# Attention in pairs of heads of two groups on halves of the array, with TensorE's order written by hand

## The chip, the cores and the metric

The kernel runs on one core of a Trainium2 chip. TensorE (PE) multiplies into PSUM, VectorE (DVE), ScalarE (ACT) and GpSimd (POOL) do the rest, and SyncE (SP) issues the loads. The metric is the device time of one execution in microseconds (us); lower is better.

## The reference

It is one layer of a decoder trunk on 512 tokens of width 1024: RMSNorm, one wide input projection, three branches (RG-LRU, native sparse attention, gated linear attention), a gated merge, an output projection and a SwiGLU network. The change is in the attention, of 16 heads of width 64 in 4 groups of 4; the heads of a group share keys and values. Each head has three branches with their own keys and values, added under gates:

```python
logit_c = einsum("bgrsd,bgcd->bgrsc", q, kc) + bias_c            # 31 compressed blocks
o_cmp = softmax(where(valid_c, logit_c, NEG_INF)) * valid_c @ vc
o_slc = softmax(q @ k_slc + bias, causal) @ v_slc                # all earlier blocks at this length
o_win = softmax(q @ k_win + bias, window of 256) @ v_win
o = g[0] * o_cmp + g[1] * o_slc + g[2] * o_win                   # g = sigmoid(gate)
```

## The kernel before

All products keep float32 precision: weights and activations are split into a high and a low part, and `mm3` adds three products of parts (high by high, high by low, low by high), at 512 moving columns for most. Weights come in pieces of 128x1024 numbers (`piece`): SP loads one, ACT makes the high part (line 93), POOL during the attention the low part (line 94), three buffers of each.

The stage that the change touches lasts from about 98 to 413 us. It runs over 4 groups `g`, 4 blocks `qb` of 128 queries and 2 pairs `rp` of heads of the group: 32 steps of two heads each. A block has `n1` = 128, 256, 384 or 512 selected keys, `nw` = 128 to 384 keys of the window and 32 compressed ones; the last two kinds are scored together, in `n2` = `nw` + 32 columns. One step is:

- `att_scores`, for each head: two products into bank `s1` and two into `s2` (lines 550 and 551). The stationary operand is the queries, high part over low part, on all 128 rows of the array; the keys move, and their high part stands twice, once for each half of the rows. The second product, queries' high part by keys' low part, has only the 64 rows of the group's half (`half`). Then for each branch DVE adds the bias and takes the maximum (line 558, which frees the bank), and ACT takes the exponential with its sum (line 560). DVE makes the reciprocal of the sums, times the gate (lines 562 and 563), and scales the selected probabilities and the compressed ones (lines 568 and 571), POOL those of the window (line 570).
- `att_out`, of the step before: PE transposes the probabilities in blocks of 128x128 (lines 597 and 602) into one of two `pt` banks, DVE or, each third time, ACT copies them out (`psb`, line 606), and the products with V (lines 620 and 623) use 64 columns of the array each: selected blocks on the left half, window and compressed ones on the right half, 256 columns of two heads at once. ACT and DVE add the halves (lines 635 and 636).
- `fill`: between these stand steps of other projections from `feed` (keys, values and queries of the later groups and the merge gates: 9 jobs of 16 steps, a step being three products of 512 columns, or six of 256 in the values' job). A job takes both banks of `pg` and is copied out at its end.

The program only gives priorities by the order of the code; a scheduler puts each engine's instructions in order. PSUM has 8 banks: 2 in `pg` (projections), 3 in `pa` (scores), 2 in `pt` (transposes), 1 in `po` (sums of V).

Of the kernel before, what the change touches and what calls it, by code (L numbers as in the profile page):

```python
# [22 lines left out]
EV = 3  # L23
# [11 lines left out]
# Distance lines: entry j is the bias at distance JMAX - j (WMAX - j in the window's), NEG where masked.  # L35
# [4 lines left out]
ORDER = "sos"  # L40
RATE = [0.8, 0.8, 0.8, 0.8]
NBIAS, NP1, NP2 = 4, 4, 3
# [11 lines left out]
def bias_select():  # L54
    """[33, LINE + WLINE] one-hot rows: which bucket (or the mask row 32) each line entry takes."""
# [9 lines left out]
def hybrid_block_kernel(ctx, tc, x, rel_table, norm_g, w_in, conv_w, conv_b, lru_w_gates, lru_b_gates,  # L65
# [59 lines left out]
    def psum_t(pools=None):  # L125
        return [p.tile([128, S], F32, name="gps", tag=t) for p, t in (pools or ((pg, "g"), (pg, "g")))]

    def psum_tok():
        ps = [pg.tile([128, 2, 256], F32, name="gps", tag="g") for _ in range(2)]
        return [ps[tb // 2][:, tb % 2] for tb in range(TB)]  # L130

    def steps_t(ps, pc_, kh, act):
        (h, l), (ah, al) = pc_, act
        for n in range(2):
            c = slice(n * 128, n * 128 + 128)
            for k in range(4):
                mm3(ps[n], h[:, k, c], l[:, k, c], ah[:, kh * 4 + k], al[:, kh * 4 + k],
# [3 lines left out]
    def steps_tok(ps, pc_, kh, act):  # L141
        (h, l), (ah, al) = pc_, act
        for tb in range(TB):
# [25 lines left out]
    def gemm_tok(ch, act):  # L169
        """Four [128 tokens, 256 columns] tiles."""  # L170
# [25 lines left out]
    def rstd_of(ss, n, pool):  # L196
        """(ss / n + EPS) ** -0.5, one Newton step on top of the table's square root."""
# [29 lines left out]
    pg = psum_ctx.enter_context(tc.tile_pool(name="pg", bufs=2, space=PSUM))  # L227
    pa = psum_ctx.enter_context(tc.tile_pool(name="pa", bufs=3, space=PSUM))
# [216 lines left out]
    def feed(jobs):  # L445
# [12 lines left out]
        for i, (jb, kh) in enumerate(todo):  # L458
# [5 lines left out]
            if kh:  # L464
                evac(ps)
# [755 lines left out]
```

## Time and profile before

| | us |
|---|---|
| median of 3 runs (lowest, highest) | 1343.72 (1341.64, 1348.01) |
| span of the profiled execution | 1345.8 |
| PE busy in it | 1309.2 (97%) |
| attention in it, from 98 to 413 us | 315.0 |
| in the attention: PE, DVE, ACT, POOL busy | 309.8, 214.1, 170.5, 83.8 |

The table is read by stages: the share of busy time is a mean, and the change is in one stage. A busy PE is not a PE at its peak, since an instruction's length includes its way through the array and what it waits for there. What an instruction takes from PE is the distance from its start to the next start.

### The profile page before, as it was taken

The page shows a single profiled execution, that of the slowest core. Times are in us where ns is not written, and L with a number is a line of the kernel's source. Part 1 is how long each engine was busy: PE and PEld are TensorE (multiplying, and loading weights), DVE is VectorE, ACT ScalarE, POOL GpSimd, SP SyncE. Part 2 cuts the span into 40 slices and gives each one's busy share as a digit, 9 for nine tenths or more (in the row PEclk, how much of TensorE's full clock was granted, in tenths as well). Part 3 has the DMA queues.
Part 4 walks back from the last instruction along what each step waited for, and adds up shares of the span by engine and source line. Part 5 has one row for each costly group of instructions (what it writes and reads, how often), then busy time and mean ns, then how long its engine had stood idle before and what let it go on. Part 6 is the DMA issues. An engine that isn't in the chain of part 4 may idle for free.

```text
span 1345.8 us, 17422 instructions
## 1 busy us (share of the span) xinstructions
PE 1309.2 (97%) x6648; PEld 1038.9 (77%) x6648; DVE 675.3 (50%) x1362; ACT 558.5 (41%) x1057; POOL 332.8 (25%) x219
## 2 busy tenths in 40 slices
PE   7999999999999999989999999999999999999997
PEld 6885556655557877878998888889998888887886
DVE  6536867566667799774333212444743333331114
ACT  4335555456755555844342323323433232231222
POOL 1221323232231454223122133220112222222220
PEclk9998999989999989989999999999999999999999
DMA  7920211103112222333222233534223333332331
GB/s 233 272 67 16 87 32 32 32 16 86 32 33 72 79 71 78 98 94 76 68 78 78 79 94 94 163 103 151 86 75 98 94 94 94 94 99 89 97 105 66
DMA packets 139716, 117.97 MB, mean 88 GB/s; under 512 B 8338, under 2 KB 129406, under 8 KB 139632
## 3 DMA queue, kind: packets, MB, share of 16 engines
q1 hardware_dynamic: 139040, 115.81, 29.4%
q8 instruction: 52, 0.85, 0.3%
q10 hardware_dynamic: 592, 1.05, 0.2%
q14 instruction: 32, 0.26, 0.1%
HBM read 114.67 MB, written 2.17 MB: 87 GB/s over the span
## 4 chain that ended last, share of the span: by engine, by line
PE 81%; DVE 11%; issue 3%; ACT 3%; POOL 2%; DMA 0%; DVEq 0%; ACTq 0%; POOLq 0%
PE gps L163 24%; PE gps L166 12%; PE gps L121 7%; PE gps L123 6%; PE gps L122 6%; PE ops L623 3%; PE acc L121 3%; PE acc L122 3%; PE s L551 3%; PE acc L123 3%; PE ptp L602 3%; PE s L550 3%; DVE xc L822 1%; DVE p L568 1%; DVE wlo L94 1%
## 5 line engine op out<-in xcount | busy, mean ns | idle before, releaser
L94 POOL TENSOR_TENSOR wlo<-wraw,whi 128x1024 fp32r<-128x1024 f32 x90 | 220.2, 2447 | 634.1 <-ACT whi L93 352.1
L93 ACT CAST whi<-wraw 128x1024 fp32r<-128x1024 f32 x177 | 185.3, 1050 | 408.3 <-PE gps L166 262.9
L163 PE MATMUL gps<-hh,whi 128*128 128x512 f32 x704 | 278.2, 396 | 5.6 <-ACT whi L93 3.0
L166 PE MATMUL gps<-hl,whi 128*128 128x512 f32 x704 | 277.1, 394 | 0.0
L94 DVE TENSOR_TENSOR wlo<-wraw,whi 128x1024 fp32r<-128x1024 f32 x87 | 113.7, 1308 | 271.6 <-PE gps L163 148.4
L163 PE MATMUL gps<-hh,wlo 128*128 128x512 f32 x704 | 175.7, 392 | 4.4 <-DVE wlo L94 4.4
L163 PEld LDWEIGHTS gps<-hh,whi 128*128 128x128 f32 x704 | 134.3, 191 | 35.2 <-ACT whi L93 3.9
L163 PEld LDWEIGHTS gps<-hh,wlo 128*128 128x128 f32 x704 | 133.1, 189 | 32.6 <-DVE wlo L94 4.8
L166 PEld LDWEIGHTS gps<-hl,whi 128*128 128x128 f32 x704 | 134.2, 191 | 28.8 <-issue 1.1
L560 ACT ACTIVATE p<-p,mx 128x384 f32<-128x384 f32 (+3 forms) x128 | 69.8, 546 | 67.9 <-DVE mx L558 66.6
L121 PE MATMUL gps<-whi,hh 128*128 128x256 f32 x320 | 94.0, 294 | 0.8 <-DVE kl L475 0.8
L122 PE MATMUL gps<-wlo,hh 128*128 128x256 f32 x320 | 93.1, 291 | 0.0
L123 PE MATMUL gps<-whi,hl 128*128 128x256 f32 x320 | 91.8, 287 | 0.0
L121 PE MATMUL gps<-hh,whi 128*128 128x512 f32 (+1 forms) x184 | 79.4, 436 | 2.6 <-ACT hh L223 1.5
L163 PE MATMUL gps<-yh,whi 128*128 128x512 f32 x192 | 75.7, 394 | 2.7 <-ACT whi L93 2.7
L166 PE MATMUL gps<-yl,whi 128*128 128x512 f32 x192 | 75.4, 393 | 0.0
L121 PE MATMUL acc<-whi,ah 128*128 128x512 f32 x176 | 68.6, 390 | 0.8 <-DVE fsg L1140 0.8
L123 PE MATMUL gps<-hh,wlo 128*128 128x512 f32 (+1 forms) x184 | 68.6, 374 | 0.0
L122 PE MATMUL gps<-hl,whi 128*128 128x512 f32 (+1 forms) x184 | 68.6, 374 | 0.0
L123 PE MATMUL acc<-whi,al 128*128 128x512 f32 x176 | 68.5, 389 | 0.0
L122 PE MATMUL acc<-wlo,ah 128*128 128x512 f32 x176 | 68.5, 389 | 0.0
L570 POOL TENSOR_TENSOR p<-p,sc 128x768 f32<-128x768 f32 (+2 forms) x32 | 40.4, 1264 | 104.1 <-DVE sc L563 74.7
(320 smaller groups left out, 2273.9 us busy)
## 6 DMA issues: line engine op xcount, KB each, us to landing
wraw<-in_w_in_dram SPq DMA_DIRECT2D x68, 512.0 KB, 3.8
wraw<-in_w_ffn_in_dram SPq DMA_DIRECT2D x88, 256.0 KB, 3.2
wraw<-in_w_ffn_out_dram SPq DMA_DIRECT2D x22, 512.0 KB, 3.7
wraw<-in_w_in_dram SPq DMA_DIRECT2D x32, 256.0 KB, 3.1
wraw<-in_w_branch_dram SPq DMA_DIRECT2D x16, 512.0 KB, 3.4
wraw<-in_w_branch_dram SPq DMA_DIRECT2D x16, 256.0 KB, 4.1
wraw<-in_w_out_dram SPq DMA_DIRECT2D x8, 512.0 KB, 3.5
bias<-line_d SPq DMA_DIRECT2D x12, 256.0 KB, 4.3
```

The costliest lines, as they stand in the source:

```text
L93: a_.copy(hi, raw)
L94: lo_eng.tensor_tensor(lo, raw, f(hi), op=OP.subtract)
L121: pe.matmul(ps, lh, rh, start=first, stop=False)
L122: pe.matmul(ps, lh, rl, start=False, stop=False)
L123: pe.matmul(ps, ll, rh, start=False, stop=last)
L163: pe.matmul(ps[n], part_[:, k, c], ah[:, kk], start=kk == 0 and part_ is h, stop=kk == 7 and part_ is l)
L166: pe.matmul(ps[n], h[:, k, c], al[:, kk], start=False, stop=False)
L550: pe.matmul(s[:, :n], q[:, r, qs], kh[:, sl], start=True, stop=False)
L551: pe.matmul(s[:, :n], q[half, r, qs], kl[half, sl], start=False, stop=True)
L560: a_.activation(o, o, AF.Exp, scale=-1.0, bias=mx[:, br, j:j + 1], accum_out=sm[:, br, j:j + 1])
L570: g_.tensor_tensor(w_, w_, sc[:, 2][:, :, None].to_broadcast([128, 2, nw]), op=OP.mult)
L602: pe.transpose(tps[:, hf, j], src[:, j], ident)
```

## The change

It pairs heads in another way. A step now has one head `r` of two groups, 2`gp` and 2`gp`+1. The queries of the first stand in rows 0 to 63, those of the second in rows 64 to 127, high and low part in two tiles; the keys stand once (`KH`, `KL`), the first group's in the upper half of the rows and the second's in the lower. Each score bank takes three products of 64 rows instead of one of 128 and one of 64, and the two heads' products alternate on the two halves of the rows, each head into its own bank: 12 products of one shape (64 rows, 128 columns) in a row. In `att_out` each head has its half of the array's columns for all three branches, 128 moving columns at a time, all products of a step in a row of one shape (128 rows, 64 columns); the compressed ones use the full 128 rows with a mask in `VC`. The sums of the four query blocks of a pair of heads stay in one bank and are copied out once (line 621), so nothing is left to add. The compressed probabilities have four fixed tiles `PC`, set to zero once.

POOL now scales the selected probabilities too. The steps run over 2 pairs of groups, 4 heads and the blocks in the order 0, 3, 1, 2. TensorE's order is that of the code (`manual_schedule`): scores of step i, V products of step i - 2, half of the filling steps, then the transposes of step i - 1 with the other filling steps between. `RATE` is 4.6 filling steps to a step. The banks are 1 in `pg`, 4 in `pa`, 2 in `pt`, 1 in `po`: a projection tile is copied out after 8 filling steps, and the next one uses the same bank. Three pieces of weights are loaded ahead instead of two, and the queries' weights come in four loads of 64 columns instead of one of 256. Biases are loaded per pair of heads.

```diff
-ORDER = "sos"
-RATE = [0.8, 0.8, 0.8, 0.8]
-NBIAS, NP1, NP2 = 4, 4, 3
+QORD = (0, 3, 1, 2)
+RATE = 4.6
+NQ, NP1, NP2, NPSB, NBIAS = 4, 3, 3, 5, 4
...
-    pg = psum_ctx.enter_context(tc.tile_pool(name="pg", bufs=2, space=PSUM))
-    pa = psum_ctx.enter_context(tc.tile_pool(name="pa", bufs=3, space=PSUM))
+    pg = psum_ctx.enter_context(tc.tile_pool(name="pg", bufs=1, space=PSUM))
+    pa = psum_ctx.enter_context(tc.tile_pool(name="pa", bufs=4, space=PSUM))
...
+        for i, (segs, evac, tok) in enumerate(jobs):
+            two = pcs[2 * i:2 * i + 2]
+            for n in range(2):
+                ps = pg.tile([128, S], F32, name="gps", tag="g")
...
+                evac(ps, n)
...
+    def k_evac(gp):
+        def evac(ps, n):
+            c = slice((0, S + 32)[n], (S, 2 * S + 32)[n])
+            a_.copy(KH[gp][:, c], ps)
+            v_.tensor_tensor(KL[gp][:, c], ps, f(KH[gp][:, c]), op=OP.subtract)
...
-                pe.matmul(s[:, :n], q[:, r, qs], kh[:, sl], start=True, stop=False)
-                pe.matmul(s[:, :n], q[half, r, qs], kl[half, sl], start=False, stop=True)
...
+        for s, sl, n in ((s1, slice(0, n1), n1), (s2, sl2, n2)):
+            for i, (qp, kk) in enumerate(((0, kh), (0, kl), (1, kh))):
+                for gi, h in enumerate(HALF):
+                    pe.matmul(s[gi][:, :n], q[h, qp, qs], kk[h, sl], start=i == 0, stop=i == 2)
...
-        for j in range(2):
-            v_.tensor_scalar(p1[:, j, :n1], p1[:, j, :n1], sc[:, 1, j:j + 1], None, op0=OP.mult)
-        w_ = p2[:, :, :nw]
-        g_.tensor_tensor(w_, w_, sc[:, 2][:, :, None].to_broadcast([128, 2, nw]), op=OP.mult)
...
+        for o, br, n in ((p1[:, :, :n1], 1, n1), (p2[:, :, :nw], 2, nw)):
+            g_.tensor_tensor(o, o, sc[:, br][:, :, None].to_broadcast([128, 2, n]), op=OP.mult)
...
-                    pe.matmul(oo, VV[gp][:, kb, c:c + 64], psb[:, hf], start=rp == 0 and i_ == 0, stop=last)
...
+                    v, m = VV[gp][:, kb, c:c + 64], p[:, gi]
+                pe.matmul(ops[h, qb * 128:qb * 128 + 128], v, m, start=first and i == 0,
+                          stop=last and i == len(blocks) - 1)
+        if last:
+            v_.tensor_copy(yb[:, gp, r].rearrange("p (b c) -> p b c", b=TB),
+                           ops.rearrange("p (b c) -> p b c", b=TB)[:, :, ::-1])
...
+    with tc.manual_schedule(engines={mybir.EngineType.PE}):
+        for i in range(len(its) + 2):
+            if i < len(its):
+                gp, r, qb = its[i]
+                probs[i] = att_scores(*its[i])
...
+            if i >= 2:
+                att_out(*its[i - 2], turned.pop(i - 2))
+            quota += RATE
+            n = int(quota)
+            quota -= n
+            for _ in range((n + 1) // 2):
+                next(work, None)
+            n -= (n + 1) // 2
+            if 0 < i <= len(its):
+                turned[i - 1] = []
+                for _ in att_turn(*its[i - 1], probs.pop(i - 1), turned[i - 1]):
+                    if n:
+                        n -= 1
+                        next(work, None)
```

PE, before, in a block with 512 selected keys of the second pair of groups: a head's scores, one filling step (lines 121 to 123), V products of two blocks, transposes.

```order
L550 MATMUL s_2833<-kh_248,q 128x512
L551 MATMUL s_2833<-kl_250,q 128x512
L550 MATMUL s_2834<-kh_248,q 128x416 [waits DVE_49]
L551 MATMUL s_2834<-kl_250,q 128x416
L121 MATMUL gps<-hh,whi 128x512
L122 MATMUL gps<-hl,whi 128x512
L123 MATMUL gps<-hh,wlo 128x512
L623 MATMUL ops<-psb,vv_252 64x256 [waits DVE_49]
L623 MATMUL ops<-psb,vv_252 64x256
L602 MATMUL ptp<-ident,p_2705 128x128 [waits PE_49]
L602 MATMUL ptp<-ident,p_2705 128x128
```

PE, after, in a block with 384 selected keys: the second half of a step's scores, then all V products of an earlier step (line 618; `kh` and `kl` are the keys' parts, `vv` and `vc` the values).

```order
L555 MATMUL s_1505<-kh_247,q 128x416
L555 MATMUL s_1506<-kh_247,q 128x416
L555 MATMUL s_1505<-kl_249,q 128x416
L555 MATMUL s_1506<-kl_249,q 128x416
L555 MATMUL s_1505<-kh_247,q 128x416
L555 MATMUL s_1506<-kh_247,q 128x416
L618 MATMUL ops<-psb,vv_251 64x128 x8
L618 MATMUL ops<-psb,vv_251 64x128 [waits Activation_49]
L618 MATMUL ops<-psb,vv_251 64x128 x3
L618 MATMUL ops<-psb,vv_251 64x128 [waits DVE_49]
L618 MATMUL ops<-psb,vv_251 64x128
L618 MATMUL ops<-psb,vc 64x128 x2
```

The shapes no longer alternate: six products of 64 rows follow each other, two heads by turns, and then 16 of 64 columns.

DVE, before, at the end of a step: a copy of transposes, the reciprocal, the scaling, and the first bias of the next step.

```order
L606 COPY psb<-ptp 128x512 [waits PE_49]
L562 RECIPROCAL sc<-sm 128x6 [waits Activation_49]
L563 TENSOR_TENSOR sc<-sc,gates 128x6 [waits DVE_49]
L568 TENSOR_SCALAR p_2705<-p_2705,sc 128x384 [waits DVE_49]
L610 COPY psb<-ptp 64x128 [waits PE_49]
L568 TENSOR_SCALAR p_2705<-p_2705,sc 128x384
L571 TENSOR_TENSOR pc<-pc,sc 128x2x23
L558 ISA p_2788,mx<-s_2795,bias 128x512 [waits PE_49]
```

DVE, after, at the end of a step.

```order
L567 RECIPROCAL sc<-sm 128x6 [waits Activation_49]
L569 TENSOR_TENSOR sc<-sc,gates 128x6 [waits DVE_49]
L575 TENSOR_TENSOR pc_255<-pc_255,sc 128x2x15 [waits DVE_49]
L600 COPY psb<-ptp 128x512 [waits PE_49] x2
L600 COPY psb<-ptp 128x384 [waits PE_49]
L564 ISA p_1498,mx<-s_1503,bias 128x384 [waits PE_49,Pool_49]
```

The two scalings of line 568 are gone, and all three copies of the transposes of the step before now stand behind the reciprocal, which waits for ACT's exponentials.

ACT, before, where a tile of keys of the later groups (line 473) is copied out of the projection's bank, between the exponentials of two heads.

```order
L560 ACTIVATE p_1471,sm<-p_1471,mx 128x512 [waits DVE_49]
L560 ACTIVATE p_1472,sm<-p_1472,mx 128x384 [waits DVE_49]
L560 ACTIVATE pc,sm<-pc,mx 128x31 [waits DVE_49]
L473 CAST kh_248<-gps 64x512 [waits PE_49]
L560 ACTIVATE p_1471,sm<-p_1471,mx 128x512 [waits DVE_49]
L560 ACTIVATE p_1472,sm<-p_1472,mx 128x384 [waits DVE_49]
L560 ACTIVATE pc,sm<-pc,mx 128x31 [waits DVE_49]
```

ACT, after, where such a tile (line 471) is copied out: the exponentials of both heads of step 5 stand ahead of it.

```order
L566 ACTIVATE p_1322,sm<-p_1322,mx 128x512 [waits DVE_49,Activation_49]
L566 ACTIVATE p_1322,sm<-p_1322,mx 128x512 [waits DVE_49]
L566 ACTIVATE p_1323,sm<-p_1323,mx 128x384 [waits DVE_49] x2
L566 ACTIVATE pc_257,sm<-pc_257,mx 128x31 [waits DVE_49] x2
L471 CAST kh_248<-gps 128x512 [waits PE_49]
L600 COPY psb<-ptp 128x128 [waits PE_49]
```

PE, after, at the same place: the last of the eight filling steps of that tile, then the first of the next tile, which uses the same bank and so waits for DVE's part of the copying out; behind it stand transposes of step 4.

```order
L121 MATMUL gps<-hh,whi 128x512
L122 MATMUL gps<-hl,whi 128x512
L123 MATMUL gps<-hh,wlo 128x512
L121 MATMUL gps<-hh,whi 128x512 [waits DVE_49]
L122 MATMUL gps<-hl,whi 128x512
L123 MATMUL gps<-hh,wlo 128x512
L595 MATMUL ptp<-ident,p_1236 128x128 [waits Pool_49]
L595 MATMUL ptp<-ident,p_1236 128x128
```

The copying out has moved behind the whole step's exponentials, and in PE's fixed order the next tile stands right behind the one that is to be copied out.

## Rows read from the trace of the kernel before

**Rows 1.** The page of the profile, its first part: for each engine busy time, share of the span and instructions (PE is TensorE, DVE VectorE, ACT ScalarE, POOL GpSimd).

```profile
PE 1309.2 (97%) x6648; PEld 1038.9 (77%) x6648; DVE 675.3 (50%) x1362; ACT 558.5 (41%) x1057; POOL 332.8 (25%) x219
```

**Rows 2.** Busy time by stretch: start and end, length, then busy time (and instructions) of PE, its weight loads, DVE, ACT and POOL, the granted clock, and the share and rate of the DMA. The attention, and two stretches inside it in which the clock was at its lower level.

```profile
98.00:413.00 315.00, 309.75 (x1508) 186.97 (x1507) 214.09 (x686) 170.50 (x489) 83.78 (x77) 0.96 0.14 40
...
262.60:276.30 13.70, 13.59 (x39) 8.56 (x40) 6.71 (x29) 5.83 (x20) 1.30 (x2) 0.50 0.16 39
395.70:399.20 3.50, 3.50 (x16) 1.57 (x14) 1.71 (x10) 2.85 (x7) 0.00 (x0) 0.51 0.25 87
```

**Rows 3.** The timeline of PE alone, 12 us in the middle of the attention: start, length, line, out<-in, rows*columns of the array, then the columns that move (the last number of 128x512). The time that an instruction takes from PE is the difference of two starts, since the lengths overlap.

```profile
300.55 0.51 PE L550 MATMUL s<-kh,q 128*128 128x512 f32 x1
300.99 0.49 PE L551 MATMUL s<-kl,q 64*128 64x512 f32 x1
301.41 0.45 PE L550 MATMUL s<-kh,q 128*128 128x416 f32 x1
301.79 0.45 PE L551 MATMUL s<-kl,q 64*128 64x416 f32 x1
302.17 0.50 PE L121 MATMUL gps<-hh,whi 128*128 128x512 f32 x1
302.51 0.40 PE L122 MATMUL gps<-hl,whi 128*128 128x512 f32 x1
302.74 0.39 PE L123 MATMUL gps<-hh,wlo 128*128 128x512 f32 x1
302.98 1.03 PE L602 MATMUL ptp<-ident,p 128*128 128x128 f32 x8
303.77 0.47 PE L121 MATMUL gps<-hh,whi 128*128 128x512 f32 x1
...
308.50 0.40 PE L123 MATMUL gps<-hh,wlo 128*128 128x512 f32 x1
308.83 0.65 PE L623 MATMUL ops<-psb,vv 128*64 128x256 f32 x4
309.41 0.30 PE L597 MATMUL ptp<-ident,pc 128*64 128x128 f32 x1
...
311.12 0.44 PE L620 MATMUL ops<-psb,vc 64*64 64x128 f32 x4
311.48 0.50 PE L550 MATMUL s<-kh,q 128*128 128x512 f32 x1
```

**Rows 4.** Groups of instructions by line between 98 and 413 us: line, engine, operation, out<-in, shapes, count, busy time in all and mean of one in ns, idle time before them.

```profile
L560 ACT ACTIVATE p<-p,mx 128x384 f32<-128x384 f32 (+3 forms) x128 | 69.8, 546 | 67.9 <-DVE mx L558 66.6
...
L568 DVE TENSOR_SCALAR p<-p,sc 128x128 f32<-128x128 f32 (+3 forms) x64 | 53.3, 869 | 0.6
L623 PE MATMUL ops<-psb,vv 128*64 128x256 f32 x304 | 53.1, 413 | 2.1 <-DVE psb L606 2.1
...
L570 POOL TENSOR_TENSOR p<-p,sc 128x768 f32<-128x768 f32 (+2 forms) x32 | 40.4, 1264 | 104.1 <-DVE sc L563 74.7 <-DVE mx L558 26.1 <-ACT psb L606 2.3
L94 POOL TENSOR_TENSOR wlo<-wraw,whi 128x1024 fp32r<-128x1024 f32 x16 | 38.6, 2414 | 16.3 <-ACT whi L93 7.3 <-DVE mx L558 4.7 <-DVE q L499 4.2
...
L606 DVE COPY psb<-ptp 128x512 f32<-128x512 f32 x47 | 31.8, 688 | 22.8 <-PE ptp L602 22.3
...
L560 ACT ACTIVATION_READ_ACCUMULATOR p<-p,mx 128x1 f32 x128 | 24.0, 187 | 0.0
L560 ACT ACTIVATE pc<-pc,mx 128x7 f32<-128x7 f32 (+3 forms) x64 | 19.0, 296 | 7.7 <-DVE mx L558 7.7
...
L620 PE MATMUL ops<-psb,vc 64*64 64x128 f32 x128 | 15.9, 296 | 0.0
...
L752 ACT ACT_TABLE_LOAD x6 | 7.7, 1283 | 0.1
```

**Rows 5.** The same groups with the shapes kept apart, ACT.

```profile
L560 ACT ACTIVATE p<-p,mx 128x384 f32<-128x384 f32 x48 | 29.3, 611 | 11.0 <-DVE mx L558 10.4
...
L560 ACT ACTIVATE p<-p,mx 128x512 f32<-128x512 f32 x16 | 11.6, 724 | 24.9 <-DVE mx L558 24.8
...
L498 ACT ACTIVATE q<-gps 64x512 fp32r<-64x512 f32 x12 | 7.1, 592 | 5.8 <-PE gps L123 3.4 <-DVE q L499 2.2
```

**Rows 6.** The timeline of all engines around 260 us (PEld is a weight load; in brackets the idle time before, and what ended it).

```profile
259.63 3.02 DVE L568 TENSOR_SCALAR p<-p,sc 128x128 f32<-128x128 f32 x2
...
260.21 2.36 POOL L94 TENSOR_TENSOR wlo<-wraw,whi 128x1024 fp32r<-128x1024 f32 x1
...
260.94 0.50 PE L121 MATMUL gps<-hh,whi 128*128 128x512 f32 x1
261.04 0.19 PEld L122 LDWEIGHTS gps<-hl,whi 128*128 128x128 f32 x1
261.27 0.40 PE L122 MATMUL gps<-hl,whi 128*128 128x512 f32 x1
...
261.74 0.27 PE L602 MATMUL ptp<-ident,p 128*128 128x128 f32 x1
...
262.71 0.90 PE L602 MATMUL ptp<-ident,p 128*128 128x128 f32 x3 [0.69 <-DVE p L568]
```

**Rows 7.** Who PE waited for between 98 and 413 us: in all, times, longest.

```profile
PE ptp L602 <- DVE p L568: 3.1, 3, 1.4
PE ops L623 <- DVE psb L606: 2.1, 2, 1.9
```

More of the change, by code (lines that the diff above doesn't have):

```diff
@@ new lines, in gate_job, with evac, do @@
+    def gate_job(c):
+        def evac(ps, n):
+            (v_.tensor_copy if n else a_.copy)(M[:, 2 * c + n], ps)
+        return [(MERGE + D + c * 256, 256)], evac, False
+    def do(jb):
+        segs, evac, tok = jb
+        ch = chunk(w_in, 0, INW, segs)
+        if tok:
+            ps = [p.tile([128, 2, 256], F32, name="gps", tag=t) for p, t in gpools]
+            both = [ps[tb // 2][:, tb % 2] for tb in range(TB)]
+            for kh in range(2):
+                for _ in steps_tok(both, ch[kh], kh, hT):
+                    pass
+        else:
+            ps = gemm_t(ch, hT)
+        for n in range(2):
+            evac(ps[n], n)
@@ L519, in dims, with load_bias @@
+    state["ev"] = 0
+    def load_bias(gp, r):
+        for gi in range(2):
+            b = ap_.tile([128, S + 384], F32, name="bias", bufs=NBIAS)
+            base = ((2 * gp + gi) * R + r) * (LINE + WLINE)
+            sy.dma_start(b[:, 0:S], dap(line_d, base, [[1, 128], [1, S]]))
+            sy.dma_start(b[:, S:S + 384], dap(line_d, base + LINE, [[1, 128], [1, 384]]))
+            biases[gp, r, gi] = b
     def dims(qb):
@@ L592, in tr, with att_turn @@
+        po_ = pc[:, 2 * gp * 32:2 * gp * 32 + 64].rearrange("p (g c) -> p g c", g=2)[:, :, :nv]
+        v_.tensor_tensor(po_, po_, sc[:, 0][:, :, None].to_broadcast([128, 2, nv]), op=OP.mult)
+        return p1, p2, pc
+    def att_turn(gp, r, qb, probs, out):
+        p1, p2, pc = probs
+        n1, nw, k0 = dims(qb)
+        blocks = [("s", kb) for kb in range(qb + 1)] + [("w", kb) for kb in range(k0 // 128, qb + 1)] + [("c", 0)]
+        for u in range(0, len(blocks), 2):
             tps = pt.tile([128, 2, 2, 128], F32, name="ptp", tag="pt")
-            psb = ap_.tile([128, 2, 2, 128], F32, name="psb", bufs=3)
@@ L617, in pv, with att_out @@
+            yield
+    opss = {}
+    def att_out(gp, r, qb, blocks):
+        first, last = qb == QORD[0], qb == QORD[-1]
+        if first:
+            opss[0] = po.tile([128, S], F32, name="ops", tag="o")
+        ops = opss[0]
+        for i, (kind, kb, p) in enumerate(blocks):
+            for gi, h in enumerate(HALF):
                 if kind == "c":
-                    js = (kb,) if qb < 3 else (0, 1)
-                    for j in js:
-                        pe.matmul(oo[:, j], VC[g][:, j], psb[0:64, 1, 0], start=False, stop=last and j == js[-1])
+                    v, m = VC[:, 2 * gp + gi], p[:, 0]
@@ L621, in pv @@
                 else:
                     c = (0 if kind == "s" else 128) + gi * 64
-                    pe.matmul(oo, VV[gp][:, kb, c:c + 64], psb[:, hf], start=rp == 0 and i_ == 0, stop=last)
-        n = max(len(left), len(right))
-        t = tr(0)
-        for i in range(n):
-            nxt = tr(i + 1) if i + 1 < n else None
-            yield
-            pv(*t)
-            t = nxt
-        if rp == 1:
-            half = slice(gi * 64, gi * 64 + 64)
-            t_o = ap_.tile([64, R, 128], F32, name="t_o", bufs=2)
-            a_.copy(t_o, ops[64:128])
-            v_.tensor_tensor(yb[half, gp, :, qb * 128:qb * 128 + 128], ops[0:64, :, ::-1], t_o[:, :, ::-1], op=OP.add)
@@ L652, in hybrid_block_kernel @@
     biases = {}
-    for r in range(R):
+    for r in range(2):
         load_bias(0, r)
     ge0 = cmp_mlp(0, hids[0])
-    xp1 = cmp_blocks(1, x2[:, 1])
+    xp1 = cmp_blocks(1, x2[1])
     do(v_job(0))
```

285 lines of the change are left out of this document (102 added, 183 removed).

## Prediction

> **What bounds the kernel now.** I first read the engines' shares: PE is busy for 97% of the span and no other engine for more than half [rows 1]. Since a share is a mean over stages, I then read the stretch that the change touches. In the 315 us of the attention PE is busy for 309.8, DVE for 214, ACT for 171, POOL for 84 [rows 2], and PE waits for others for some 5 us [rows 7]. So PE sets the stage; the question is what fills its time, and the busy time does not tell, since lengths overlap. I take distances of starts [rows 3]. The reader is to see three things there. In a run of one shape a product of 512 columns takes 0.23 us (302.51, 302.74, 302.98), so 0.45 ns a column, and eight transposes take 0.79 (0.109 each, the last hidden). Where the shape changes with each product, as from 300.55, the same width takes 0.44, and the first product after the last change still 0.34: five products that would take 1.07 us by width take 1.96, with four changes, 0.22 each. And four entries of line 623 (two halves of the columns, each product in two passes) take 0.58 at 256 columns, four of line 620 at 128 columns 0.36: the difference, 0.22, is two pair passes of 128 columns, so 0.11 each, and 0.14 belongs to entering and leaving; with 0.10 on the product before (308.50) and 0.11 after, the two changes cost 0.35. I take 0.2 us for a change of shape.
>
> **Check on the time before.** Filling: 144 steps, 128 of three products of 512 and 16 of six of 256: 384 x 0.231 + 96 x 0.118 = 100 us. Scores: 16 heads x 2560 columns x 2 products x 0.45 ns = 37. Transposes: 304 x 0.109 and 32 half ones = 35. V: 304 entries [rows 4], two at a time, so 152 pair passes of 256 columns at 0.22, and 64 of 128 at 0.11 = 40. Changes: along PE's order I count 480; x 0.2 = 96. Waits 5. The clock is 0.96 of full over the stage [rows 2], so 12 us are lost to its lower level. The sum is 325 for 315 measured: 3% high, good enough. The point is the 96: changes of shape cost nearly as much as all the filling.
>
> **The change, part by part, on PE.** *Filling* stays: 100 us. *Scores*: 3 x 2560 x 8 pairs of heads = 61,440 columns, if the two heads run at the same time on their halves of the rows: 28 us, and 2 more for the 128- and 160-column products, for which I take no less than a transpose's 0.109: 30. No row shows row halves at work together; column halves do [rows 3]. The bounds are 30 and, one half after the other, 56. I take 30, by the column halves as the nearest rows. *Transposes*: 304 and 32 whole ones: 336 x 0.109 = 37. *V*: 19 blocks of selected and window keys in the four query blocks of a pair of heads, x 8, and 32 compressed ones: 184 pairs, two passes, 368 x 0.11 = 40. *Changes*: three in each of 32 steps, 96 x 0.2 = 19. PE's own work is 226 us at full clock instead of some 308.
>
> Here a rule of the skill speaks against the sum. The rows show that a weight load of 0.19 us runs under a product on the same rows of the array: line 122's load starts at 261.04, in line 121's product, and its own product starts at 261.27, after 512 columns and the 0.10 of a change [rows 6]; from 302.51 on no load shows at all [rows 3]. The Trainium skill, "TensorE: Matmul & The Clock Gate", Part 3, "The mechanism", says that a weight load overlaps running matmuls only when the row group differs. By that rule each of the 192 score pairs would carry a load, some 0.11 us (the 0.34 after a change less 0.23), 21 us in all, and the forecast would be 1323. The trace differs from it, so I keep 30 us.
>
> **Waits that the change adds.** A projection tile now has one bank, and the next tile's first product waits until ACT and DVE have copied the last one out. Behind that product, in PE's fixed order, stand the transposes of step i - 1 and the scores of step i + 1. In ACT's order the copying out stands behind the exponentials of step i. Counted along the order there are 17 such boundaries: 4 with nothing between the last step of a tile and the first of the next, 4 with one group of transposes, 5 with two groups, 4 with the next step's scores and V products between. The place shown in the order (step 5, 512 keys): ACT's exponentials start 0.5 (first bank) and 0.69 (bias, taken as line 606's length) after the scores begin, and take 2 x 0.91 + 2 x 0.80 + 2 x 0.48 = 4.4 [rows 4, 5]; ACT's copy 0.59, then DVE's 0.69 behind the reciprocal: ready at about 7.0. PE is there after 1.3 (scores), 1.5 (V), 0.4 (changes) and 1.4 (two filling steps) = 4.6. Wait: some 2.5 us. The same sum at the others gives 2 to 3 us for the 4 adjacent ones (11 in all), 2 to 3 for the next 4 (9), 0 to 1 for the 5 (2), none for the rest: 22 us. ACT's table loads of the merge gates' sigmoid (1.28 each, two to a tile [rows 4]) now delay a tighter chain; half hidden, 6 us. DVE's sums beside POOL: a DVE instruction that reads two tiles of SBUF waits for a POOL instruction under way (line 568 took 3.02 us for two, beside a POOL split of 2.36 [rows 6]); line 568's 53 us [rows 4] go away with this change, and 3 us stay. Waits: 31 us in all, bounds 8 (the old 5, and the end of the stage) and 60.
>
> **What hides, and the clock.** POOL gets the selected probabilities: by line 570 (40 us for the windows' [rows 4]) and the ratio of the keys, 320 to 288 on average, 45 us more, on an engine with 84 us of work in a stage that stays above 230. The transposes of a step come a whole step after its scores, so some 4 us of POOL are covered; if POOL's split of 2.4 us falls in front, the cover is just gone, and what then is late are transposes. The copying out of keys and queries takes half as many instructions at the same length. The queries' loads in four parts make 32 loads of 8, on SP ahead of the biases; pieces are loaded a tile ahead (8 steps, some 13 us), so I cost them at nothing; uncovered they would cost up to 5 us at the front, where a query tile is computed before the attention. The clock lost 12 us before; two stretches at the lower level, 13.7 and 3.5 us long [rows 2], lie in the stage, the first of them right at a wait of PE (262.71 [rows 6]), while PE had five waits in all [rows 7]. With more waits but a denser PE I take 16, bounds 4 and 40.
>
> **Sum.** 226 + 31 + 16 = 273 us for 315: 42 us off the profiled execution's 1345.8, which is 2 us over the median. Off the median of 1343.7: about 1302 us.
>
> **Rivals.**
> *Waits mostly hidden.* Boundaries come when the copying out is done, since PE runs late anyway: 226 + 10 + 8 = 244, 1273 us. For it: DVE loses 60 us of work. Against it: ACT's order is fixed with the exponentials ahead.
> *The chain of the other engines sets the step.* First bank 0.5, bias 0.5, exponentials 3.9 on average (128 x 0.73 and 64 x 0.48 over 32 [rows 4]), reciprocal to compressed scaling 0.7, two copies of transposes behind them 1.4, and ACT's other work (splits, copies, sigmoid) 1.7, all in a row: 8.7 us for PE's 7.1. 33 x 8.7 = 287, and 12 of clock: 299, 1328 us. For it: DVE's copies stand behind the reciprocal. Against it: ACT has gaps of over 2 us a step for its other work, and the step with most exponentials goes with the fewest transposes. (The Trainium skill, "TensorEngine Tiling (Array Packing)", PSUM Bottleneck, states this case as a rule: tiling speeds up the array, not the emptying of PSUM.)
> *Row halves don't run together.* The runs are as written, but 26 us of the gain are missing, of which some 6 come out of the waits: 1322 us.
> *Slower: the clock falls after each wait.* At each of some 17 waits the clock stays low for 8.6 us (the mean of 13.7 and 3.5): 146 us at half, 73 lost, and a longer chain of the same waits, 60: 226 + 60 + 73 = 359, 1388 us. It decides once over 130 us of the stage are at the lower level; before it was some 25.
>
> **How the numbers follow.** Forecast 1302 (1283 to 1318): 0.53. Hidden waits, about 1273: 0.14. Chain, or halves one after the other, 1318 to 1337: 0.20. Within 0.5% (about what a measurement can tell from no change, 1337 to 1350): 0.06. Slower: 0.07. The range 1266 to 1336 leaves out some 0.06 below and 0.14 above. Faster 0.87, same 0.06, slower 0.07.
>
> **What would show it.** Right: in the attention the 12 score products of a step start in pairs a few ns apart and a pair of 512 columns takes 0.23 to 0.25 us; changes number about 100; the stage takes 255 to 290 us. Waits of PE at the first product of a projection tile, ended by ACT or DVE, add up to 15 to 30 us. Wrong: pairs at 0.46 us (halves in turn), 0.34 us (a load with each pair), PE waiting before the transposes for DVE's copies in each step (the chain), or the clock low for over 60 us.

## The result, and the profile after

| | median (runs) | span of the profiled execution | attention in it |
|---|---|---|---|
| before | 1343.63 us (1341.64 to 1348.01) | 1345.8 us | 98.1 to 412.0: 313.9 us |
| after | 1291.01 us (1289.63 to 1291.54) | 1287.9 us | 94.9 to 355.4: 260.5 us |

The ratio is 0.9609, with a 95% interval of 0.9578 to 0.9639: 52.6 us less, where 42 were forecast (1302). The spans of the profiled executions differ by more than the medians, 57.9 us: a device time is some 1.7 us longer than its span (1289.63 beside 1287.9), so that of before lies some 4 us above its median and that of after 1.4 below. Of these 57.9 us the attention gave 53.4, the part ahead of it 3.2, and the rest 1.3.

The page of the profile after, the line that answers to [rows 1]:

```profile
PE 1232.6 (96%) x7068; PEld 1039.9 (81%) x7068; DVE 596.0 (46%) x1246; ACT 544.0 (42%) x1037; POOL 362.5 (28%) x223
```

Busy time by stretch after, with the columns of [rows 2]: the attention, and three short stretches inside it.

```profile
94.90:355.40 260.50, 237.95 (x1955) 191.19 (x1954) 141.95 (x584) 159.22 (x477) 116.45 (x81) 0.98 0.22 57
192.40:195.90 3.50, 3.50 (x14) 2.91 (x13) 0.01 (x1) 0.59 (x1) 0.00 (x0) 0.51 0.00 0
236.80:240.20 3.40, 3.40 (x15) 2.33 (x15) 0.00 (x0) 0.27 (x1) 3.40 (x2) 0.50 0.00 0
305.10:308.50 3.40, 3.40 (x12) 2.74 (x11) 0.00 (x0) 1.78 (x3) 1.70 (x2) 0.50 0.00 0
```

PE has 72 us less in the stage than in [rows 2] with more instructions in it, DVE 72 us less, POOL 33 us more. PE is idle for some 22 us of it, where it was for 5. The clock was at its lower level for 10.3 us, where the two stretches of [rows 2] alone had 17.2.

The timeline of PE after, 12 us of the attention with the step of the 128-key block and the next one, that of 512 keys (columns as in [rows 3]):

```profile
187.40 1.09 PE L618 MATMUL ops<-psb,vv 128*64 128x128 f32 x16
188.33 0.39 PE L618 MATMUL ops<-psb,vc 128*64 128x128 f32 x4
188.65 0.50 PE L121 MATMUL gps<-hh,whi 128*128 128x512 f32 x1
...
189.22 0.39 PE L123 MATMUL gps<-hh,wlo 128*128 128x512 f32 x1
191.76 0.50 PE L121 MATMUL gps<-hh,whi 128*128 128x512 f32 x1 [2.15 <-DVE q L493]
...
193.94 0.63 PE L122 MATMUL gps<-hl,whi 128*128 128x512 f32 x1
194.37 0.63 PE L123 MATMUL gps<-hh,wlo 128*128 128x512 f32 x1
...
197.07 0.50 PE L555 MATMUL s<-kh,q 64*128 64x512 f32 x2
197.41 0.39 PE L555 MATMUL s<-kl,q 64*128 64x512 f32 x2
197.64 0.58 PE L555 MATMUL s<-kh,q 64*128 64x512 f32 x4
198.06 0.35 PE L555 MATMUL s<-kl,q 64*128 64x416 f32 x2
```

Three things stand in it. A pair of score products of 512 columns takes 0.23 us (197.41 to 197.64): both heads in the time that [rows 3] has for one product in a run; only the first pair carries a change (0.34). Ten pair passes of V take 1.25 us (187.40 to 188.65). And after the last product of a projection tile, which starts at 189.22 and takes 0.23, PE begins nothing until 191.76, because the next tile wants the same bank, which DVE's line 493 reads last; 0.6 us later the granted clock falls to its lower level (0.51 from 192.4 to 195.9), and products of 512 columns take 0.43 (193.94 to 194.37).

Who PE waited for in the attention after (answers to [rows 7]):

```profile
PE gps L121 <- DVE q L493: 11.2, 6, 2.3
PE gps L121 <- ACT M L499: 4.3, 4, 2.4
PE gps L121 <- DVE kl L472: 1.8, 1, 1.8
PE gps L121 <- ACT vv L480: 1.4, 2, 1.2
PE ptp L595 <- DVE psb L600: 1.1, 1, 1.1
PE gps L121 <- DVE M L499: 1.0, 1, 1.0
```

The five rows of line 121 are the single bank: 19.7 us. With three rows under 1 us the sum is 22.6.

### The profile page after: what moved, and what is told of

Same layout as the page of the kernel before. It is cut to its first block, busy times and chain, and to the rows that moved or that the text cites. A ratio compares the mean times of both kernels' runs of the same rounds, so it can differ in the third digit from the quotient of the medians.

```text
span 1287.9 us, 18204 instructions
## 1 busy us (share of the span) xinstructions
PE 1232.6 (96%) x7068; PEld 1039.9 (81%) x7068; DVE 596.0 (46%) x1246; ACT 544.0 (42%) x1037; POOL 362.5 (28%) x223
## 4 chain that ended last, share of the span: by engine, by line
PE 62%; DVE 10%; ACT 4%; issue 3%; POOL 2%; DMA 0%; DVEq 0%; SPq 0%; ACTq 0%; POOLq 0%
PE gps L163 22%; PE gps L166 11%; PE gps L121 5%; PE gps L122 5%; PE gps L123 4%; PE acc L121 3%; PE acc L122 3%; PE acc L123 3%; DVE xc L799 2%; PE ops L618 1%; DVE wlo L94 1%; PE ptp L595 1%; ACT p L566 1%; POOL g L832 1%; DVE a L847 1%
## 5 line engine op out<-in xcount | busy, mean ns | idle before, releaser
L573 POOL TENSOR_TENSOR p<-p,sc 128x256 f32<-128x256 f32 (+3 forms) x64 | 76.5, 1217 | 141.8 <-DVE sc L569 99.1
L121 PE MATMUL gps<-hh,whi 128*128 128x512 f32 (+1 forms) x184 | 76.3, 419 | 22.0 <-DVE q L493 11.2
```

The source lines that it names most:

```text
L121: pe.matmul(ps, lh, rh, start=first, stop=False)
L573: g_.tensor_tensor(o, o, sc[:, br][:, :, None].to_broadcast([128, 2, n]), op=OP.mult)
```

## The experiments

The theory was that of the prediction: the gain is 380 fewer changes of shape and two heads at a time on the row halves, and the single projection bank gives some 20 us back. Against it stood: the row halves alone; DVE's relief (64 operations that scaled p1, 53.3 us in [rows 4], went to POOL); the order fixed by hand; and the chain of the other engines. Each kernel is the changed one with the edit shown, unless another is named; times are medians beside 1291.0 us. Beside each group of runs the kernel before was at 1342.5 to 1343.8 us, so a difference of one microsecond says nothing here.

| run | median, us | against after | ratio to before (95%) |
|---|---|---|---|
| e1_heads_in_turn | 1291.82 | +0.8 | 0.9611 (0.9566 to 0.9656) |
| e7_same_rows | 1315.07 | +24.1 | 0.9803 (0.9777 to 0.9828) |
| e2_v_in_turn | 1310.0 | +19.0 | 0.975 (0.9718 to 0.9783) |
| e3_broken_runs | 1313.1 | +22.1 | 0.9772 (0.974 to 0.9805) |
| e4_edge_apart | 1288.39 | -2.6 | 0.9588 (0.9553 to 0.9624) |
| e8_edge_at_end | 1271.16 | -19.9 | 0.9467 (0.9453 to 0.9481) |
| e6_order_free | 1273.67 | -17.3 | 0.9487 (0.9473 to 0.9501) |
| e10_edge_free | 1270.45 | -20.6 | 0.9473 (0.9445 to 0.9502) |
| e5_scale_on_dve | 1339.35 | +48.3 | 0.997 (0.9958 to 0.9982) |
| e9_dve_order_free | 1315.93 | +24.9 | 0.9809 (0.9784 to 0.9835) |
| e12_turn_later | 1335.98 | +45.0 | 0.9941 (0.992 to 0.9963) |
| e11_before_pool (on the kernel before) | 1345.17 | | 1.0022 (1.0003 to 1.0041) |

### Do the row halves run together?

```diff
-            for i, (qp, kk) in enumerate(((0, kh), (0, kl), (1, kh))):
-                for gi, h in enumerate(HALF):
+            for gi, h in enumerate(HALF):
+                for i, (qp, kk) in enumerate(((0, kh), (0, kl), (1, kh))):
```

> Only the order of the score products within a step changes: all three of one head (rows 0 to 63), then all three of the other (rows 64 to 127), with no other shape change and no other work. Theory (the two row halves run together, worth half of the scores' streaming): the 192 pairs have 61,440 columns per head, 25.6 us at the full clock, so the scores take 25 us more and the kernel 20 to 26 us more than the changed kernel, 1311 to 1317 us. Rival (the gain comes from the runs of one shape and from the other engines alone): within 3 us of the changed kernel.

Measured: no difference, and the rival's number. But its trace shows that the edit did not do what it was made for. The timeline of PE, a step of 512 keys:

```profile
200.16 0.40 PE L555 MATMUL s<-kl,q 64*128 64x512 f32 x2
200.40 0.60 PE L555 MATMUL s<-kh,q 64*128 64x512 f32 x4
```

In the program kh, kl, kh of one head stand ahead of kh, kl, kh of the other; on the chip they still start two by two, kh with kh and kl with kl, a pair in 0.24 us. PE began the second half's product three products ahead of its place. So this run tells nothing of what the halves are worth, and the next one puts both heads on the same rows (it leaves out the second head's own scores):

```diff
-                    pe.matmul(s[gi][:, :n], q[h, qp, qs], kk[h, sl], start=i == 0, stop=i == 2)
+                    pe.matmul(s[gi][:, :n], q[HALF[0], qp, qs], kk[HALF[0], sl], start=i == 0, stop=i == 2)
```

> Both heads' scores are taken from the first head's rows (0 to 63), so that the two products of a pair stand on the same half of the array; this leaves out the second head's own scores. Number, shape and order of all instructions stay. When the heads were only listed one after the other, the second half's products still began beside the first's, so that order alone does not part them. Theory (row halves run side by side): 61,440 columns at the full clock in turn, 24 to 28 us more than the changed kernel, 1315 to 1319 us, and the scores' own time 62 to 66 us for 38. Rival (the halves take turns anyway and the trace's starts mislead): within 3 us.

```profile
212.48 0.63 PE L555 MATMUL s<-kl,q 64*128 64x512 f32 x2
212.95 0.99 PE L555 MATMUL s<-kh,q 64*128 64x512 f32 x4
```

The same view of this run: a pair now takes 0.47 us (212.48 to 212.95). The scores' time, as the sum of the distances of starts over the stage, is 68.0 us for 38.0, two more than the 62 to 66 expected, and those of the projections and transposes, which hold the waits, sum to 5 less. The kernel is 24.1 us longer, as the theory had it. The row halves run side by side, and this is worth 24 us.

### And the column halves of V?

```diff
-        for i, (kind, kb, p) in enumerate(blocks):
-            for gi, h in enumerate(HALF):
+        for gi, h in enumerate(HALF):
+            for i, (kind, kb, p) in enumerate(blocks):
```

> Only the order of the V products within a step changes: all blocks of one head (columns 0 to 63), then all of the other (columns 64 to 127). Theory (the column halves run together, 368 pair passes of 0.109 us): 40 us more than the changed kernel, about 1331 us. Rival (halves of columns are not worth anything beyond the saved shape changes): within 3 us.

Measured 19 us, between the two. The timeline of PE shows why, in a step with seven blocks (14 passes) a head, whose last block is vc:

```profile
137.57 1.58 PE L618 MATMUL ops<-psb,vv 128*64 128x128 f32 x14
138.93 0.27 PE L618 MATMUL ops<-psb,vc 128*64 128x128 f32 x1
138.99 0.27 PE L618 MATMUL ops<-psb,vv 128*64 128x128 f32 x1
139.04 0.27 PE L618 MATMUL ops<-psb,vc 128*64 128x128 f32 x1
```

Of the 14 vv entries ahead of the first vc, 12 are the first head's and two already the second's; the next ones alternate. The second half starts some four passes ahead of its place and then goes on alone. So listing halves one after the other costs what lies beyond that reach: V's distances sum to 74.1 us for 46.6, 27.5 more, and 8 come back elsewhere, 5 of them in shorter waits. The pairing counts, and for runs of three products a half the listing does not.

### What does a change of shape cost?

```diff
             for gi, h in enumerate(HALF):
                 ...
                 pe.matmul(ops[h, qb * 128:qb * 128 + 128], v, m, start=first and i == 0,
                           stop=last and i == len(blocks) - 1)
+            if i < nf:
+                next(work, None)
```

> The projection steps that stand behind the V products of a step are put between them, one behind each of the first two or three pairs: 144 more changes of tile shape on TensorE (244 for 100), the same products. Theory (a change costs 0.2 us): 29 us more, less some 3 us of bank waits that a V pair now covers: 1311 to 1320 us, and the row halves and column halves still run together. Rival (changes cost little, the pairing is the whole gain): within 5 us of the changed kernel.

Measured 22.1 us more, inside the theory's bounds. The timeline of PE, where a projection step now stands between V pairs:

```profile
206.50 0.44 PE L618 MATMUL ops<-psb,vv 128*64 128x128 f32 x4
206.87 0.50 PE L121 MATMUL gps<-hh,whi 128*128 128x512 f32 x1
207.20 0.39 PE L122 MATMUL gps<-hl,whi 128*128 128x512 f32 x1
207.43 0.40 PE L123 MATMUL gps<-hh,wlo 128*128 128x512 f32 x1
207.76 0.44 PE L618 MATMUL ops<-psb,vv 128*64 128x128 f32 x4
```

A V pair takes 0.37 for its 0.22, the product after it 0.33 and the one before the next pair 0.33 for 0.23: 0.35 in all for two changes, 0.175 each. The sums agree: V's and the projections' distances, without those over 0.7 us, take some 25 us more, over 144 changes, 0.174. By that price the 380 changes that went are worth 66 us, an estimate, since only changes between V and projections were priced; the prediction's 0.2 gave 77.

### Is the wait for the bank worth its length?

The first edit stops a run of projection steps at a tile's end and issues the evacuation with the tile's last product:

```diff
+    def run(n):
+        for j in range(n):
+            if j and state["edge"]:
+                return n - j
+            next(work, None)
+        return 0
...
-                    if n:
+                    if n and not state["edge"]:
```

> No new projection tile is begun in the run of steps in which the tile before it ended: the steps left over come after the transposes or after the next step's scores, and the tile's evacuation is issued with its last product. 100 changes of shape as now. Theory (the single bank gives back some 20 us in 10 waits of 1.5 to 2.8 us at the first product of a tile): 12 to 20 us less than the changed kernel, 1271 to 1279 us, and the waits at the first product of a tile under 5 us. Rival (the wait is the chain of the other engines, and comes up at the scores or transposes when it goes here): within 5 us of the changed kernel.

Only 2.6 us, as the rival had it. Who PE waited for:

```profile
PE gps L121 <- DVE q L503: 6.3, 5, 2.2
PE ptp L605 <- ACT psb L610: 3.0, 3, 2.1
PE ptp L599 <- DVE psb L610: 2.7, 4, 1.0
PE ptp L605 <- DVE psb L610: 2.6, 3, 1.1
```

The bank's part fell from 19.7 to 8.7, but the transposes, which had waited 1.6, now wait 8.6 for the copies of the transposes ahead of them; the rule had also taken away steps that stood between them. At 13 of the 17 places where one tile follows another only transposes stood between the two, and these places hold 8.3 of the bank's 8.7 us. The second edit keeps the steps between the transposes and makes all 18 tiles end with a step of the attention:

```diff
-            quota += RATE
-            n = int(quota)
-            quota -= n
+            n = (8 if i // 4 in (1, 7) and i % 4 > 1 else 4) if i < len(its) else 0
```

> Each step of attention gets 4 projection steps (8 in four of the 32), so that all 18 projection tiles end with a step, ahead of the next step's scores and V products; steps stay between the transposes, and a tile's evacuation is issued with its last product. 98 changes of shape. Theory (waits for the single bank are worth their 20 us where the work between two tiles covers the evacuation and nothing else loses its cover): waits at a tile's first product under 4 us, waits at the transposes as in the changed kernel (1 to 3 us), 1271 to 1279 us. Rival (the chain of the other engines sets the pace and the wait only moves, as it did in the run with the edge apart): transposes wait 8 us or more, within 5 us of the changed kernel.

```profile
PE ptp L601 <- ACT psb L606: 3.6, 3, 1.8
PE ptp L601 <- DVE psb L606: 2.0, 2, 1.1
PE ptp L595 <- DVE psb L606: 1.5, 2, 0.8
PE gps L121 <- DVE q L499: 1.2, 3, 0.5
```

The theory's time, at the lower end of its range: 19.9 us less, with 1.2 us left at the bank; at all 17 places scores and V products now stand between the tiles. All waits together are 10.0 us for 22.6, and the granted clock is 0.99 in the stage. So 12.6 of the 19.9 us are waits; that the sum is so near to the bank's 19.7 is in part chance. The transposes wait 7.1, not the 1 to 3 of the theory and little less than in the first edit, so keeping the steps between them did not give their cover back. What parts the two edits is the bank, 8.7 us for 1.2. A chain of the other engines did not set the pace, or the time would not have fallen; why the transposes wait in both was not looked into.

### The fixed order

```diff
-    with tc.manual_schedule(engines={mybir.EngineType.PE}):
+    with ExitStack():
```

> TensorE's order is no longer fixed by hand; the scheduler places its products, with all else as changed: 120 changes of shape for 100 (counted in the built program). Theory (what counts is the number of changes, at some 0.17 us each by the run with broken runs, and the waits): 3 us for the changes, the waits within 6 us of now, so 1286 to 1300 us. Rival (the fixed order is where the gain is): 20 us more or above, 1311 us.

It is 17.3 us *shorter*, outside the bounds of both. Who PE waited for:

```profile
PE gps L121 <- DVE q L493: 2.9, 5, 1.1
PE gps L121 <- ACT M L499: 1.4, 2, 1.0
```

The bank's waits are 5.7 us (four rows) in place of 19.7, at 120 changes for 100: the scheduler splits runs of scores (41 runs for 33) and one of V, and has more work between the end of a tile and the start of the next: only transposes at 4 places for 9, nothing at none for 4. The fixing of the order was thus no part of the gain; as it was written it cost what the bank gave away. With both edits:

> The 4 projection steps to a step of attention of the run with all edges at a step's end, and TensorE's order left to the scheduler; 104 changes of shape. Theory (both remove the same bank waits of some 20 us, so that little is left to add): 1266 to 1274 us, within 5 us of either alone. Rival (the free order's gain is another one, at the transposes, and adds up): 1250 to 1262 us.

It came out at 1270.45, the theory's case: the two edits remove the same waits, and together they are the best version found, level with e8_edge_at_end.

### DVE's relief

```diff
-        for o, br, n in ((p1[:, :, :n1], 1, n1), (p2[:, :, :nw], 2, nw)):
+        for gi in range(2):
+            v_.tensor_scalar(p1[:, gi, :n1], p1[:, gi, :n1], sc[:, 1, gi:gi + 1], None, op0=OP.mult)
+        for o, br, n in ((p2[:, :, :nw], 2, nw),):
             g_.tensor_tensor(o, o, sc[:, br][:, :, None].to_broadcast([128, 2, n]), op=OP.mult)
```

> The scaling of p1 goes back from POOL to DVE, in the form that the kernel before had (64 operations, 53.3 us there). Pairing, runs and order of TensorE stay. Theory (TensorE's own path decides, DVE is busy for some 160 of the stage's 260 us and has room): DVE rises to 205 to 215 us, and the kernel takes 2 to 12 us more than the changed kernel by longer waits for the bank and the probabilities. Rival (the relief of DVE is the gain): 35 us more or above, 1326 us.

48 us: the rival, and nearly the whole gain of the change. Busy time by stretch (its attention), then who PE waited for:

```profile
95.60:405.30 309.70, 255.81 (x1950) 203.23 (x1949) 202.61 (x648) 159.52 (x477) 80.60 (x49) 0.91 0.19 48
```

```profile
PE gps L121 <- DVE q L493: 20.1, 6, 6.1
PE ops L620 <- DVE psb L602: 7.9, 4, 2.6
PE ptp L597 <- DVE psb L602: 5.7, 4, 2.3
```

DVE is busy for 202.6 of 309.7 us, two thirds, and yet PE waits 53.7 us (all rows) for 22.6, and the clock falls to 0.91: some 58 us at the lower level, 29 lost, for 5. DVE's busy time is itself in good part standing still beside POOL. The timeline of POOL, DVE and PE ahead of one of PE's waits:

```profile
125.88 1.61 POOL L575 TENSOR_TENSOR p<-p,sc 128x768 f32<-128x768 f32 x1 [3.63 <-DVE sc L569]
126.08 1.62 DVE L573 TENSOR_SCALAR p<-p,sc 128x384 f32<-128x384 f32 x1
...
127.45 2.45 POOL L94 TENSOR_TENSOR wlo<-wraw,whi 128x1024 fp32r<-128x1024 f32 x1
127.63 2.33 DVE L577 TENSOR_TENSOR pc<-pc,sc 128x46 f32<-128x46 f32 x1
129.89 0.68 DVE L602 COPY psb<-ptp 128x512 f32<-128x512 f32 x1
...
130.49 0.67 DVE L493 SCALAR_TENSOR_TENSOR q<-gps,q 128x512 fp32r<-128x512 f32 x1
...
131.31 0.77 PE L121 MATMUL gps<-hh,whi 128*128 128x512 f32 x1 [4.65 <-DVE q L493]
```

The compressed scaling of 46 columns starts in POOL's split of weights (line 94) and ends 0.06 us after it; behind it stand a copy of transposes and the copying out that PE waits for. Of line 577's 32 operations, the 23 with no POOL instruction beside them took 0.16 to 0.21 us, and the nine that started in a split took 2.33 to 2.37. The scaling of p1 (line 573) does the same beside POOL's scaling of p2 (line 575), as at 126.08: with 512 columns, eight of 16 started in it and took 1.67 to 1.69 us, the other eight 0.48 to 0.49. At their median lengths without POOL beside them these two lines would need some 30 us, an estimate; they took 80. So of the 61 us by which DVE is busier than in the changed kernel, most is standing, not work. The Trainium skill, "SBUF — State Buffer", Terms, has a rule for this: DVE and GpSimd (POOL here) share one pair of ports, which an instruction holds for its whole length while the other is blocked. These operations, which work on SBUF alone, agree with it; but DVE's copies of the transposes out of PSUM (line 602, 512 columns) keep their 0.69 us in a split as without, so here not every DVE instruction is blocked. How much of the 48 us the standing makes, no run shows, since none took POOL's work from beside DVE.

Is it the order, fixed without regard to DVE?

> The scaling of p1 on DVE, as in the run that cost 48 us, but with TensorE's order left to the scheduler, which weighs the other engines' times as it places the products; 124 changes of shape. Theory A (DVE's longer work costs that much only against an order that was fixed without regard to it): within 12 us of the run with the free order alone, 1271 to 1286 us. Theory B (at 8 us a step the chain of the other engines with DVE in it sets the pace, in whatever order TensorE works): 1320 to 1345 us, with TensorE waiting 40 us or more and its clock below 0.95 in the stage.

1315.93: between the two, just below theory B's bounds and 42.3 us above the run with the free order alone; PE still waits 36.2 us, nearly all for DVE, and the clock is 0.95 in the stage, both just short of what theory B expected. The better order is worth 23 us here and does not help out of it. Is it the length of the way from the scores to the transposed probabilities?

```diff
-            if i >= 2:
-                att_out(*its[i - 2], turned.pop(i - 2))
+            if i >= 3:
+                att_out(*its[i - 3], turned.pop(i - 3))
...
-            if 0 < i <= len(its):
-                turned[i - 1] = []
-                for _ in att_turn(*its[i - 1], probs.pop(i - 1), turned[i - 1]):
+            if 1 < i <= len(its) + 1:
+                turned[i - 2] = []
+                for _ in att_turn(*its[i - 2], probs.pop(i - 2), turned[i - 2]):
```

> The run with the scaling of p1 on DVE (1339 us), with TensorE's order still fixed by hand, but the transposes of a step come two steps after its scores instead of one, and its V products three instead of two (one more buffer each for p1 and p2); the same work on every engine. Theory (with p1's scaling on it DVE needs longer than one step from the scores to the transposed probabilities, though it is busy for two thirds of the time only): waits at the transposes and V products for psb fall from 15 us to under 5, the clock stays up, 1290 to 1306 us. Rival (DVE's amount of work, or its waits beside POOL, set the pace): 1325 to 1345 us.

```profile
PE gps L121 <- DVE q L493: 22.3, 5, 7.7
PE ptp L591 <- DVE psb L602: 7.5, 5, 2.9
PE ptp L597 <- DVE psb L602: 6.6, 3, 4.0
```

No: 3.4 us, and the waits for psb are 17.9 us (with line 620's 3.8) where they were 14.8 (with line 591's 1.2). That theory falls. A likely reason, which no run isolates: the projection's copying out and the transposes' copies stand in the same DVE queue, behind whatever DVE is held up with, as at 127.63 above. Last, the same relief in the kernel before:

```diff
-        for j in range(2):
-            v_.tensor_scalar(p1[:, j, :n1], p1[:, j, :n1], sc[:, 1, j:j + 1], None, op0=OP.mult)
+        g_.tensor_tensor(p1[:, :, :n1], p1[:, :, :n1], sc[:, 1][:, :, None].to_broadcast([128, 2, n1]), op=OP.mult)
```

> The kernel before with one part of the change alone: the scaling of p1 goes from DVE to POOL (53.3 us of DVE's work); heads, halves, runs and order stay as before, 288 changes of shape as counted for the kernel before (289). Theory (with 315 us of TensorE's work DVE was not the bound there, TensorE waited 3.1 and 2.1 us for it at two lines): 0 to 8 us less, 1336 to 1344 us. Rival (the relief of DVE is itself what the change gained): 1295 to 1310 us.

```profile
98.00:413.00 315.00, 308.26 (x1542) 186.44 (x1541) 172.62 (x632) 176.75 (x497) 117.19 (x109) 0.99 0.15 41
```

DVE is at 172.6 us for 214 in the same stretch, and the time is 1.0022 of before: nothing gained, against the 0 to 8 us that were expected. (Between the profiled executions the stage itself is 7 us shorter, 306.7 for 313.9, but the clock alone accounts for that: 3.4 us at the lower level for 23.9, so 10 us less lost.) So DVE's relief is worth nothing while PE has 310 us of work in the stage, and 42 to 48 us once it has 235. Neither part makes the gain alone. How the 48 us divide between DVE's own work and its standing beside POOL stays open. No run took back the smaller parts of the change by themselves: the order of the blocks, the loads, and the halves that need no adding.

## Why the forecast was right, and where it was off

The time lies inside the range, 11 us under the forecast. The prediction took the profiled execution's 1345.8 for 2 us over the median; it is a span, so some 4 us, but the forecast was taken off the median and is not changed by it. In the stage the terms stand so; what was measured of PE's own work is the rest, 260.5 less the other rows.

| term, us | forecast | measured |
|---|---|---|
| PE's own work at the full clock | 226 | 230 |
| waits | 31 | 22.6 |
| lower clock | 16 | 5 |
| products of the next stage begun early (lines 163 and 166, ten at about 0.28) | 0 | 3 |
| stage | 273 | 260.5 |

**PE sets the stage: right, with a condition that was missed.** e11_before_pool shows that DVE did not bound the kernel before. But the move of p1's scaling to POOL was priced at next to nothing (a smaller term for DVE beside POOL), and the chain of the other engines was weighed only for the kernel with the move made. e5_scale_on_dve shows that the move carries 48 us. Without it PE waits 54 and 36 us, mostly for DVE (e5_scale_on_dve, e9_dve_order_free), which is close to what that rival described. The forecast holds by a part of the change that it did not know to be needed; in this it was lucky.

**Changes of shape: right, a little too dear.** 0.175 for 0.2 each. By the estimate of 66 us they are the largest part of what PE was spared, as forecast.

**Row halves together: right.** Pairs at 0.23 us, e7_same_rows 24.1 us for the 26 between the two bounds. No pair takes longer for a load. By the rule of the Trainium skill that the prediction weighed ("TensorE: Matmul & The Clock Gate", Part 3, "The mechanism") the pair at 197.41 would have taken 0.34, since the one ahead of it stands on the same row groups; the trace has 0.23.

**Waits: the bank was right, the rest was not there.** 19.7 us for 22 at the boundaries: 7.4 at the four adjacent ones (forecast 11), 10.9 at nine with transposes between (11), and 1.4 at one of the four with scores and V products between (none). The place worked out in the prediction waited 1.8 us for 2.5. e8_edge_at_end took 18.5 of the 19.7 away, gave 5.5 to the transposes, and was 19.9 us faster. The 6 us of sigmoid loads and 3 of DVE beside POOL were added on top; the merge gates' rows (4.3 and 1.0) are already in the 19.7, and beside that there are 2.9.

**The clock: the step that failed in size.** The 16 us rest on the 12 lost before and a guess that more waits and a denser PE nearly balance; no row priced a single wait. (The 8.6 us of the slower rival is the mean of two stretches; the stage before had a third, 6.8 us from 105.6.) After, only three waits were followed by a lower clock, those with 2.54, 2.55 and 2.81 us from start to start (at 189.22, 234.0 and 301.9), and for 3.4 us each, so 5 us went. Those at 105.9 (2.44) and 136.4 (2.16) were followed by none. This term is 11 us off, as much as the forecast; the waits' 8 and the 3 ahead of the stage are about made up by PE's own work, the early products and the profiled execution's place above its median. With e5's waits of up to 6.1 us the same clock cost 29 us: the slower rival's mechanism exists, at a point that this kernel does not reach.

**Not forecast:** 3.2 us ahead of the attention. No run looked into it.

## What to carry to other kernels

Count TensorE's changes of tile shape beside its columns: here 0.175 us each, as much as 390 columns, and grouping products of one shape was worth more than pairing heads. When such an edit takes a quarter off the bounding engine's work, the work that it moves off the second engine is no side matter: price the new, shorter step with and without that move. And where one bank is left for a stream of tiles, let tiles end where long foreign work follows: an edit that put only transposes there gained 2.6 us, one that put scores and V products there 19.9. And look at what an instruction takes with and without another engine at work beside it: here a DVE scaling of 512 columns took 0.49 us alone and 1.69 beside POOL.

## What the runs showed of the hardware that was not expected

TensorE starts products of another half of the array ahead of their place in the program: three score products ahead (e1_heads_in_turn, no time lost at all), about four V passes ahead (e2_v_in_turn). Halves need not alternate in the listing for short runs. And two waits of nearly the same length, 2.44 us from start to start at 105.9 and 2.54 at 189.22, differed in what the clock did afterwards: none of it at the lower level, and 3.4 us. The length of a wait alone does not tell: in e2_v_in_turn one of 2.54 us from start to start (318.78) was followed by none, and in e10_edge_free the clock was at its lower level for 3.4 us from 302.8 in a stage in which no start was over 1.5 us after the one before. The third is the standing of DVE beside POOL: in e5_scale_on_dve all 43 scalings that started while a POOL instruction ran ended 0.05 to 0.28 us after it (0.19 us became 2.33), while copies out of PSUM kept their length.
